# The linear half of four groups of up tiles by seven products instead of eight

## The chip, the cores and the metric

The kernel runs on one core of one Trainium2 chip. The metric is device time in microseconds (us), the median of several runs. The engines are PE (matrix products), DVE (elementwise, two operands), ACT (scalar engine: copies, activations), POOL (elementwise, off the main path) and SP (issues transfers).

## The reference

Two encoder layers over 512 tokens of width 1024. Each layer has a token mixer, a memory cross-attention, an output projection, and then a gated feed-forward part with a causal convolution of width 3 over the tokens. The change lies in this last part alone, `x + conv_ffn(rms_norm(x), ...)`:

```python
def conv_ffn(h, w_up, conv_w, conv_b, w_down):
    u = h @ w_up                                   # 512 x 1024 @ 1024 x 5632
    c = lax.conv_general_dilated(u, conv_w[:, None, :], ...) + conv_b
    a, g = jnp.split(c, 2, axis=-1)                # linear half, gate
    return (jax.nn.silu(g) * a) @ w_down           # 512 x 2816 @ 2816 x 1024
```

## The kernel before

Every float32 product is made of three matmuls on pieces: an operand is split into a high part (rounded by ACT) and a low part (the rest, by a subtraction on DVE), and PE adds high·high, high·low and low·high. So 128 weights by 512 tokens by one k tile of 128 are three matmuls of 512 columns (`product`, L387 to L389).

**Weights.** `_pieces` lists the weight pieces in the order of use, `_blocks` cuts them into blocks of up to 1024 columns. SP's queue loads a block into one of three `raw` tiles, `split_weights` makes `whi` (ACT, L255) and `wlo` (DVE, L258) of it; six such pairs exist (`WB`).

**The feed-forward part** works through 11 groups q of 256 linear columns ("ua") and 256 gate columns ("ug"), in parts of 4, 4 and 3 groups (`HALVES`). A group is two tiles n of 128 channels of each half; each tile is one PSUM bank of 128 channels x 512 tokens, summed over 8 k tiles, 24 matmuls. Its banks are taken in turn (`TURNS`, two each of mm, sm, lg, tp). `conv` then scales the bank by the row norms (DVE, L1165), takes one tap and the bias on ACT (L1167) and two taps on DVE (L1168, L1169). The gate passes SiLU (ACT, L1333), the halves are multiplied (DVE, L1334), and the result is split again for the product with `w_down` (ACT L1190, DVE L1191; tiles `mid`).

**The product with `w_down`** comes at the end of each part and is already done by a scheme of seven products in place of eight: k tiles are taken in pairs, channels in pairs, tokens in two halves of 256, and each of the seven products is three matmuls of 256 columns (`seven`, L1247), into four banks that `decode` (L1258 to L1266) puts together. It needs sums of weight quarters (`combined`: POOL L287 to L290 into `wsum`, split at L291 to L295) and sums of the groups' results (`combine`, L1198 to L1201, on POOL into `tsum`, for a part's last group on DVE; split at L1190 and L1191 into the tiles `mid2`). One channel block of 256 (c = 3 of layer 1) and all of layer 0's third part are done plainly.

**What sets the order.** PE runs in the order in which the code issues. The other engines' instructions are put in an order of their own by the framework's scheduler when the kernel is built; on each engine that order is fixed, so an instruction that waits holds up everything behind it there.

Of the kernel before, what the change touches and what calls it, by code (L numbers as in the profile page):

```python
# [11 lines left out]
F32 = mybir.dt.float32  # L12
# [9 lines left out]
S = 512  # L22
# [63 lines left out]
def _pieces():  # L86
# [6 lines left out]
    for l in range(2):  # L93
# [45 lines left out]

TURNS = ('mm', 'mm', 'sm', 'sm', 'lg', 'lg', 'tp', 'tp')  # L140
# [42 lines left out]
def trunk(ctx, tc, head_d, x_t, mem_t, wpack, cols_a_d, cols_d, conv_d, gate_d, rel_bias, diff_lambda, consts, onehot, out):  # L183
# [87 lines left out]
    done, raw_q = [0], deque()  # L271
# [6 lines left out]
    def combined(raw, n):  # L278
        pairs = n // 2
        full = lambda t: t[:, :512 * pairs].rearrange("p (j i c) -> p j i c", j=pairs, i=4)  # L280
        (h0, l0), (h1, l1) = [tuple(wp.tile([128, WTILE], F32R, name=t, tag=t, bufs=WB) for t in ("whi", "wlo"))
                              for _ in range(2)]
        r, wsum = full(raw), sum_pool[0].tile([128, WTILE], F32, name="wsum", bufs=2)
        a12, a22, a11, a21 = (r[:, :, i] for i in range(4))
        sv = wsum[:, :512 * pairs].rearrange("p (i j c) -> p i j c", i=4, j=pairs)
        s1, s2, s3, s4 = (sv[:, i] for i in range(4))
        ADD.tensor_add(s1, a21, a22)  # L287
        ADD.tensor_sub(s3, a11, a21)
        ADD.tensor_sub(s2, s1, a11)
        ADD.tensor_sub(s4, a12, s2)  # L290
        A.copy(full(h0)[:, :, :3], r[:, :, :3])  # L291
        V.tensor_sub(full(l0)[:, :, :3], r[:, :, :3], full(h0)[:, :, :3].bitcast(F32))
        m = slice(0, 512 * pairs)
        A.copy(h1[:, m], wsum[:, m])
        V.tensor_sub(l1[:, m], wsum[:, m], h1[:, m].bitcast(F32))  # L295
        out = []
        for j in range(pairs):
            own = lambda t, i: t[:, 512 * j + 128 * i:512 * j + 128 * i + 128]
            new = lambda t, i: t[:, 128 * (pairs * i + j):128 * (pairs * i + j) + 128]
# [3 lines left out]
        return out  # L303

    def make_block(raws=None):
# [9 lines left out]
        if plan[i][0][0] == "dn":  # L315
            made[i] += combined(raw, n)
# [8 lines left out]
    ADD = G  # L325


    def weights(key, by_block=False):
# [3 lines left out]
        if i + 1 < len(plan) and plan[i + 1][0][0] in ("dn", "dw"):  # L332
            limit = first_of[i + 1] + 1
# [814 lines left out]
    def ffn(pool, l, acc):  # L1148
        rB = pool.tile([128, S], F32, name="rB", bufs=1)
        sum_pool[0] = pool  # L1150
        old = list(zip(xh, xl))
        nu = [0]
# [4 lines left out]
        def up(parts, n, ops):  # L1157
            i = nu[0]
            nu[0] += 1
            p = bank(TURNS[i % 8])  # L1160
            product(p, parts, n, ops)
            return p

        def conv(p, j):
            V.tensor_mul(p, p, rB)  # L1165
            c = ctile()
            A.activation(c, p, AF.Identity, scale=cv[l][:, 2, j:j + 1], bias=cv[l][:, 3, j:j + 1])  # L1167
            V.scalar_tensor_tensor(c[:, 1:], p[:, :S - 1], cv[l][:, 1, j:j + 1], c[:, 1:], op0=ALU.mult, op1=ALU.add)  # L1168
            V.scalar_tensor_tensor(c[:, 2:], p[:, :S - 2], cv[l][:, 0, j:j + 1], c[:, 2:], op0=ALU.mult, op1=ALU.add)  # L1169
# [23 lines left out]
        left, right = blk(0, 256), blk(1, 256)  # L1193

        def combine(b2, b1, bh, bl, fh, fl, E):
            t = pool.tile([128, 2 * S], F32, name="tsum", bufs=1)
            q = [blk(i, 256) for i in range(4)]
            E.tensor_sub(t[:, q[0]], b1[:, right], b1[:, left])  # L1198
            E.tensor_sub(t[:, q[1]], b2[:, right], t[:, q[0]])
            E.tensor_sub(t[:, q[2]], b2[:, right], b1[:, right])  # L1200
            E.tensor_sub(t[:, q[3]], b2[:, left], t[:, q[1]])  # L1201
            h, lo = (pool.tile([128, 2 * S], F32R, name="mid2", bufs=9) for _ in range(2))
            for c in ((blk(0, S), blk(1, S)) if E is V else (blk(0, 2 * S),)):
                parts_of(t[:, c], h[:, c], lo[:, c])
            two = lambda hi, lw, c: (hi[:, c], lw[:, c])
            return [(fh, fl), two(bh, bl, left), two(bh, bl, right), two(h, lo, q[3]),
                    two(h, lo, q[0]), two(h, lo, q[1]), two(h, lo, q[2])]
# [4 lines left out]
        def down(base, nq, mids, pairs, tags, last, acc2):  # L1212
            first = used[0]
            whole = [plan[first + c][0][0] == "dw" for c in range(4)]
            sizes = [1 if plan[i][0][0] != "dn" else 2 for i, _, _ in order]
            live = sum(sizes[first_of[first]:done[0]])
            banks, seen = {}, [set() for _ in range(4)]

            def refill():
                nonlocal live  # L1220
                while done[0] < min(len(order), first_of[min(used[0] + 2, len(plan))]) and live + sizes[done[0]] <= WB:
                    live += sizes[done[0]]
                    make_block()

            def start(c):
                assert plan[used[0]][0][1:] == (l, base, c)
                used[0] += 1
                if whole[c] and l == 0:
                    banks[c] = [bank("lg"), bank("tp")]
                else:  # L1230
# [213 lines left out]
```

## Time and profile before

| | |
|---|---|
| median of 3 runs | 1149.71 us (1149.57 to 1151.2) |
| the profiled execution's own time | 1150.36 us |
| its span in the trace | 1148.5 us, granted clock 0.999 |
| PE busy | 1142.7 us, 99% |
| DVE busy | 871.2 us, 76% |
| ACT busy | 592.0 us, 52% |
| POOL busy | 193.2 us, 17% |

The spans of the trace leave about 1.9 us of the run's time outside. The feed-forward part of layer 0 lies at about 240 to 600 us, that of layer 1 at about 775 to 1144 us. A matmul's own span in the trace overlaps the next one's, so what a matmul costs is read from the distance of starts and not from its span. In groups of instructions the last two columns are busy time and mean of one, and the idle time ahead of them on that engine with what ended it.

### The profile page before, as it was taken

Reading aid. Unit: us, or ns where it says so; the run is one execution under the profiler, and the core shown is the slowest. Engines: PE = TensorE matmul, PEld = TensorE weight load, DVE = VectorE, ACT = ScalarE, POOL = GpSimd, SP = SyncE. Lnnn points to the kernel's source line nnn. Section 1 sums busy time; section 2 is a strip of 40 time slices with the busy share of each in tenths; the row PEclk is TensorE's granted clock in tenths of the full one; section 3 lists DMA queues with packets and bytes.
Section 4 is the critical chain, followed back from the end, with each engine's and each line's share of the span. In section 5 each row is a group of like instructions: output and inputs, shape, how many; then the busy total and the mean of one; then the engine's idle time right before and its main releaser. Section 6 shows DMA issues by size and latency. Waiting matters only on the chain.

```text
span 1148.5 us, 16655 instructions
## 1 busy us (share of the span) xinstructions
PE 1142.7 (99%) x6311; PEld 985.1 (86%) x6311; DVE 871.2 (76%) x1455; ACT 592.0 (52%) x1032; POOL 193.2 (17%) x230
## 2 busy tenths in 40 slices
PE   9999999999999999999999999999999999999998
PEld 7888888888899888988888888988888988899887
DVE  8576778688789677977677637777887977797777
ACT  6676686555454354434457634535644444453442
POOL 0000000001543125500000000000135403360340
PEclk9999999999999999999999999999999999999999
DMA  9522242133214322343252220333241342234212
GB/s 293 173 83 84 78 142 74 58 109 110 92 57 146 111 77 80 96 144 100 69 182 70 100 94 12 101 125 119 74 126 40 127 149 74 61 91 143 92 46 102
DMA packets 39662, 117.83 MB, mean 103 GB/s; under 512 B 4767, under 2 KB 7256, under 8 KB 39582
## 3 DMA queue, kind: packets, MB, share of 16 engines
q1 hardware_dynamic: 39150, 116.37, 31.8%
q8 instruction: 50, 0.82, 0.3%
q10 hardware_dynamic: 432, 0.39, 0.1%
q14 instruction: 30, 0.25, 0.1%
HBM read 112.54 MB, written 4.21 MB: 102 GB/s over the span
## 4 chain that ended last, share of the span: by engine, by line
PE 99%; DMA 0%; DVE 0%; ACT 0%; issue 0%
PE ps_mm L365 6%; PE ps_mm L367 6%; PE ps_mm L366 6%; PE ps_mm L387 6%; PE ps_mm L388 6%; PE ps_mm L389 6%; PE ps_lg L1247 5%; PE ps_sm L388 5%; PE ps_sm L389 5%; PE ps_sm L387 5%; PE ps_mm L1247 4%; PE ps_tp L388 4%; PE ps_lg L388 4%; PE ps_tp L387 4%; PE ps_lg L387 4%; PE ps_tp L389 4%
## 5 line engine op out<-in xcount | busy, mean ns | idle before, releaser
L258 DVE TENSOR_TENSOR wlo<-raw,whi 128x1024 fp32r<-128x1024 f32 (+4 forms) x174 | 194.2, 1127 | 77.0 <-ACT whi L255 76.4
L255 ACT CAST whi<-raw 128x1024 fp32r<-128x1024 f32 (+4 forms) x174 | 168.0, 976 | 124.2 <-PE ps_sm L388 29.8
L365 PE MATMUL ps_mm<-whi,xsh 128*128 128x512 f32 (+2 forms) x328 | 126.2, 385 | 0.0
L367 PE MATMUL ps_mm<-whi,xsl 128*128 128x512 f32 (+2 forms) x328 | 123.0, 375 | 0.0
L366 PE MATMUL ps_mm<-wlo,xsh 128*128 128x512 f32 (+2 forms) x328 | 122.8, 374 | 0.0
L387 PE MATMUL ps_mm<-xsh,whi 128*128 128x512 f32 x278 | 109.3, 393 | 0.0
L388 PE MATMUL ps_mm<-xsl,whi 128*128 128x512 f32 x278 | 108.4, 390 | 0.0
L389 PE MATMUL ps_mm<-xsh,wlo 128*128 128x512 f32 x278 | 108.2, 389 | 0.0
L387 PE MATMUL ps_sm<-xsh,whi 128*128 128x512 f32 x218 | 84.8, 389 | 0.0
L388 PE MATMUL ps_sm<-xsl,whi 128*128 128x512 f32 x218 | 84.8, 389 | 0.0
L389 PE MATMUL ps_sm<-xsh,wlo 128*128 128x512 f32 x218 | 84.8, 389 | 0.0
L365 PEld LDWEIGHTS ps_mm<-whi,xsh 128*128 128x128 f32 x328 | 61.7, 188 | 11.4 <-issue 1.0
L367 PEld LDWEIGHTS ps_mm<-whi,xsl 128*128 128x128 f32 x328 | 61.7, 188 | 11.3
L366 PEld LDWEIGHTS ps_mm<-wlo,xsh 128*128 128x128 f32 x328 | 61.8, 188 | 10.1
L387 PE MATMUL ps_lg<-xsh,whi 128*128 128x512 f32 x160 | 62.2, 389 | 0.0
L388 PE MATMUL ps_lg<-xsl,whi 128*128 128x512 f32 x160 | 62.2, 389 | 0.0
L389 PE MATMUL ps_lg<-xsh,wlo 128*128 128x512 f32 x160 | 62.2, 389 | 0.0
L387 PE MATMUL ps_tp<-xsh,whi 128*128 128x512 f32 x160 | 62.2, 389 | 0.0
L388 PE MATMUL ps_tp<-xsl,whi 128*128 128x512 f32 x160 | 62.2, 389 | 0.0
L389 PE MATMUL ps_tp<-xsh,wlo 128*128 128x512 f32 x160 | 62.2, 389 | 0.0
L389 PEld LDWEIGHTS ps_mm<-xsh,wlo 128*128 128x128 f32 x278 | 52.2, 188 | 11.0
L387 PEld LDWEIGHTS ps_mm<-xsh,whi 128*128 128x128 f32 x278 | 52.2, 188 | 10.8 <-issue 0.3
(382 smaller groups left out, 2835.4 us busy)
## 6 DMA issues: line engine op xcount, KB each, us to landing
raw<-in_wpack_dram SPq DMA_DIRECT2D x178, 512.0 KB, 3.5
xt<-in_x_t_dram SPq DMA_DIRECT2D x15, 256.0 KB, 5.2
raw<-in_wpack_dram SPq DMA_DIRECT2D x15, 256.0 KB, 3.1
raw<-in_wpack_dram SPq DMA_DIRECT2D x8, 384.0 KB, 3.0
xres<-xt SPq DMA_DIRECT2D x8, 256.0 KB, 3.2
xt<-xres SPq DMA_DIRECT2D x8, 256.0 KB, 5.8
out_dram<-xt SPq DMA_DIRECT2D x7, 256.0 KB, 2.0
bt<-bias_d SPq DMA_DIRECT2D x6, 256.0 KB, 4.1
```

What stands on the lines that cost most here:

```text
L255: ins = A.copy(hi[:, c], raw[:, c])
L258: V.tensor_sub(lo[:, c], raw[:, c], hi[:, c].bitcast(F32))
L365: mm(p, sh[k][:, blk(b)], hi, start=k == 0, stop=False)
L366: mm(p, sh[k][:, blk(b)], lo, start=False, stop=False)
L367: mm(p, sl[k][:, blk(b)], hi, start=False, stop=k == KT - 1)
L387: mm(p, hi[:, blk(n)], bh, start=i == first, stop=False)
L388: mm(p, hi[:, blk(n)], bl, start=False, stop=False)
L389: mm(p, lo[:, blk(n)], bh, start=False, stop=i == last)
L1247: mm(banks[c][b][:, h], w, v, start=b not in seen[c], stop=m == nq - 1 and t == 2 and i in close)
```

## The change

In both layers, for the groups 5, 6, 8 and 9 (eight pieces in all, `SEVEN`), the linear half's product with the tokens is done by the same scheme of seven. Of its 8 k tiles two (6 and 7) stay plain, and the six others form three pairs of seven products of three matmuls of 256 columns (`up_by_seven`). Both channel tiles of the piece come out together, from four banks; ACT copies half a bank, DVE makes four additions of 256 and two of 512 columns, and `conv` of both tiles follows. The gate's two tiles follow behind on PE.

The scheme needs sums of token halves for the three k pairs. They are made once a layer in groups 0 and 1 (`token_sums`, places in `SUMS_AT`): for each pair two scaled copies on ACT, four subtractions on POOL, and two splits of 512 columns on ACT and DVE. They stay in SBUF in 12 half-size tiles `vs`.

The weight sums of a block are issued one block ahead (`block_sums`, called from `ahead`), and POOL's additions are held in the order of the code. The operand splits of a group's result sums are not issued at once but behind the third `conv` that follows (`later`, `behind`); `tsum` is gone (its sums share `wsum`), and there are 8 `mid2` tiles in place of 9. The feed-forward part takes its banks in turn throughout (`take`), also in the product with `w_down`, and one count of live weight blocks (`live`, `refill`, `release`) governs their preparation across both products.

```diff
-                piece(("ua", l, q), "w_up", l, K8, (256 * q, 256 * q + 256))
-                piece(("ug", l, q), "w_up", l, K8, (DFF + 256 * q, DFF + 256 * q + 256))
+                for key, c in ((("ua", l, q), 256 * q), (("ug", l, q), DFF + 256 * q)):
+                    piece(key, "w_up", l, (6, 7, 4, 5, 0, 1, 2, 3) if key in SEVEN else K8, (c, c + 256))
...
+SEVEN = [("ua", l, q) for l in range(2) for q in (5, 6, 8, 9)]
+SUMS_AT = {1:(4,5),2:(0,1),3:(2,3)}
...
     def ahead():
...
+        i = order[done[0]][0] if done[0] < len(order) else None
+        if i is not None and by_seven(i) and done[0] not in summed:
+            summed[done[0]] = block_sums(raw_q[0], order[done[0]][1], int(plan[i][0][0] != "dn" and first_of[i] == done[0]))
+
+    def g_sums(items):
+        for op, o, x, y in items:
+            tc.keep_in_program_order(getattr(G, "tensor_" + op)(o, x, y))
...
+        def up_by_seven(i):
+            b, seen = take(4), set()
+            where = [(2, left), (0, left), (0, right), (1, left), (3, right), (2, right), (3, left)]
+            for m, ks in enumerate(((6, 7), (4, 5), (0, 1), (2, 3))):
+                while len(made) <= i or len(made[i]) <= m:
+                    refill()
+                part = made[i][m]
+                if m == 0:
+                    for n in range(2):
+                        product(b[n], part, n, [tokens[k] for k in ks], range(2), 99)
+                else:
+                    for r in steps:
+                        c, h = where[r]
+                        (hi, lo), (vh, vl) = part[r], sums_of[ks][r]
+                        for t, (w, v) in enumerate(((hi, vh), (hi, vl), (lo, vh))):
+                            mm(b[c][:, h], w, v, start=c > 1 and c not in seen, stop=m == 3 and t == 2 and r in (2, 5, 6, 3))
+                            seen.add(c)
+                if m % 2:
+                    release(i, 2, m == 3)
+            u, w = ctile(), ctile()
+            A.copy(u[:, left], b[2][:, left])
+            V.tensor_add(w[:, right], u[:, left], b[2][:, right])
+            V.tensor_add(u[:, right], w[:, right], b[3][:, right])
+            V.tensor_add(w[:, left], w[:, right], b[3][:, left])
+            V.tensor_add(w[:, right], u[:, right], b[3][:, left])
+            V.tensor_add(b[0], b[0], u)
+            V.tensor_add(b[1], b[1], w)
+            return b[:2]
...
+            if later:
+                convs[0] += 1
+                if convs[0] == 3:
+                    convs[0] = 0
+                    behind(first, final)
...
-            t = pool.tile([128, 2 * S], F32, name="tsum", bufs=1)
+            t = [ctile(), ctile()] if E is V else [sum_tile()]
...
+        def token_sums(ks):
+            (bh, bl), (fh, fl) = (tokens[k] for k in ks)
+            tiles = [split_tiles(pool, "vs", 12) for _ in range(2)]
...
+            combine(scaled(ks[0]), scaled(ks[1]), None, None, None, None, G, parts)
...
+                    if n == 0:
+                        at[key] = begin((key, l, q))
+                        if (key, l, q) in SEVEN:
+                            cs[key] = [conv(p, j + i) for i, p in enumerate(up_by_seven(at[key]))]
```

On PE, the start of group 5's linear piece in layer 0. Before (its first tile's bank is `ps_lg_4024`; `xsh` and `xsl` are the tokens' high and low parts, names with numbers are single buffers):

```order
L387 MATMUL ps_lg_4024<-xsh_2496,whi_3885 128x512
L388 MATMUL ps_lg_4024<-xsl_2497,whi_3885 128x512
L389 MATMUL ps_lg_4024<-xsh_2496,wlo_3886 128x512
L387 MATMUL ps_lg_4024<-xsh_2506,whi_3885 128x512
L388 MATMUL ps_lg_4024<-xsl_2507,whi_3885 128x512
L389 MATMUL ps_lg_4024<-xsh_2506,wlo_3886 128x512
```

It goes on like this for 24 matmuls, and then the gate's tile follows.

And the same piece now, where its plain products (L407 to L409) of the second tile end and the products by seven begin (L1233; `vsh` and `vsl` are token sums, the third bank is `ps_tp_4099`):

```order
L407 MATMUL ps_lg_4098<-xsh_2648,whi_3917 128x512
L408 MATMUL ps_lg_4098<-xsl_2649,whi_3917 128x512
L409 MATMUL ps_lg_4098<-xsh_2648,wlo_3918 128x512
L1233 MATMUL ps_lg_4097<-xsh_2564,whi_3917 128x256
L1233 MATMUL ps_lg_4097<-xsl_2565,whi_3917 128x256
L1233 MATMUL ps_lg_4097<-xsh_2564,wlo_3918 128x256
L1233 MATMUL ps_lg_4097<-xsh_2564,whi_3919 128x256
L1233 MATMUL ps_lg_4097<-xsl_2565,whi_3919 128x256
L1233 MATMUL ps_lg_4097<-xsh_2564,wlo_3920 128x256
L1233 MATMUL ps_tp_4099<-xsh_2588,whi_3917 128x256
L1233 MATMUL ps_tp_4099<-xsl_2589,whi_3917 128x256
L1233 MATMUL ps_tp_4099<-xsh_2588,wlo_3918 128x256
```

The first 12 matmuls of the piece are 512 columns wide, the 63 others 256, and the third bank is touched first after 12 + 6 of them.

On DVE, the `conv` of the same group's first linear tile. Before, with the operand split of group 4's sums (`mid_4009`) ahead of it and the gate's tile behind:

```order
L1165 TENSOR_TENSOR ps_lg<-ps_lg,rB 128x512
L1191 TENSOR_TENSOR mid_4009<-tsum,mid_4008 128x1024
L1168 SCALAR_TENSOR_TENSOR cvo<-ps_lg,cv_81,cvo 128x511
L1169 SCALAR_TENSOR_TENSOR cvo<-ps_lg,cv_81,cvo 128x510
L1165 TENSOR_TENSOR ps_lg<-ps_lg,rB 128x512
L1168 SCALAR_TENSOR_TENSOR cvo<-ps_lg,cv_81,cvo 128x511
L1169 SCALAR_TENSOR_TENSOR cvo<-ps_lg,cv_81,cvo 128x510
```

Now, from the additions (L1239 to L1244) on, with two weight splits (L309, L312) among them, then both linear tiles (`ps_lg`) and the gate's first (`ps_mm`):

```order
L1239 TENSOR_TENSOR cvo<-cvo,ps_tp 128x256
L1240 TENSOR_TENSOR cvo<-cvo,ps_tp 128x256
L1241 TENSOR_TENSOR cvo<-cvo,ps_tp 128x256
L309 TENSOR_TENSOR wlo<-raw,whi 128x2x384
L312 TENSOR_TENSOR wlo<-wsum,whi 128x1024
L1242 TENSOR_TENSOR cvo<-cvo,ps_tp 128x256
L1243 TENSOR_TENSOR ps_lg<-ps_lg,cvo 128x512
L1244 TENSOR_TENSOR ps_lg<-ps_lg,cvo 128x512
L1248 TENSOR_TENSOR ps_lg<-ps_lg,rB 128x512 x2
L1248 TENSOR_TENSOR ps_mm<-ps_mm,rB 128x512
L1251 SCALAR_TENSOR_TENSOR cvo<-ps_lg,cv_81,cvo 128x511 x2
L1252 SCALAR_TENSOR_TENSOR cvo<-ps_lg,cv_81,cvo 128x510 x2
```

The additions are new, the split of group 4's sums has gone behind these rows (four rows further down), and the gate's first scaling stands ahead of the linear tiles' last taps.

On DVE, the end of layer 0's second part (group 7 and the start of the product with `w_down`), from the last `conv` on. Before (the last group's sums at L1198 to L1201, both halves of their split in one row at the end):

```order
L292 TENSOR_TENSOR wlo<-raw,whi 128x2x384
L1165 TENSOR_TENSOR ps_tp<-ps_tp,rB 128x512
L295 TENSOR_TENSOR wlo<-wsum,whi 128x1024
L1168 SCALAR_TENSOR_TENSOR cvo<-ps_tp,cv_81,cvo 128x511
L1169 SCALAR_TENSOR_TENSOR cvo<-ps_tp,cv_81,cvo 128x510
L1334 TENSOR_TENSOR cvo<-cvo 128x512
L1198 TENSOR_TENSOR tsum<-cvo 128x256
L1200 TENSOR_TENSOR tsum<-cvo 128x256
L1199 TENSOR_TENSOR tsum<-cvo,tsum 128x256
L1191 TENSOR_TENSOR mid<-cvo,mid 128x256
L1201 TENSOR_TENSOR tsum<-cvo,tsum 128x256
L292 TENSOR_TENSOR wlo<-raw,whi 128x2x384
```

It goes on with the two halves of the split (`L1191 ... mid_4504<-tsum,mid_4503 128x512 x2`) and a weight split (L295). Now, from the first weight split behind the last `conv`'s scaling on:

```order
L312 TENSOR_TENSOR wlo<-wsum,whi 128x1024
L1251 SCALAR_TENSOR_TENSOR cvo<-ps_sm,cv_81,cvo 128x511
L1252 SCALAR_TENSOR_TENSOR cvo<-ps_sm,cv_81,cvo 128x510
L1448 TENSOR_TENSOR cvo<-cvo 128x512
L1287 TENSOR_TENSOR cvo<-cvo 128x256 x2
L1279 TENSOR_TENSOR mid<-cvo,mid 128x256
L1287 TENSOR_TENSOR cvo<-cvo 128x256
L309 TENSOR_TENSOR wlo<-raw,whi 128x2x384
L1287 TENSOR_TENSOR cvo<-cvo 128x256
L1279 TENSOR_TENSOR mid_4698<-cvo,mid_4697 128x512
L312 TENSOR_TENSOR wlo<-wsum,whi 128x1024
L1279 TENSOR_TENSOR mid_4698<-cvo,mid_4697 128x512
```

The weight split L312 now stands between the two halves of the last split (`mid_4698`). Ahead of the last scaling stands, in the order now, the operand split of group 6's sums (1024 columns), which before was 14 rows ahead of it.

More of the change, by code (lines that the diff above doesn't have):

```diff
@@ L285, in combined @@
[L285 to L293, printed above, removed]
+        if plain:
+            c = slice(0, 512 * plain + 384)
+            split_weights(c, raw, h0, l0)
+        else:
+            A.copy(full(h0)[:, :, :3], r[:, :, :3])
+            V.tensor_sub(full(l0)[:, :, :3], r[:, :, :3], full(h0)[:, :, :3].bitcast(F32))
@@ L314, in make_block @@
             made.append([])
-        if plan[i][0][0] == "dn":
-            made[i] += combined(raw, n)
+        if by_seven(i):
+            made[i] += combined(raw, summed.pop(done[0] - 1), n, int(plan[i][0][0] != "dn" and not made[i]))
         else:
@@ L1150, in ffn, with take, refill @@
         sum_pool[0] = pool
-        old = list(zip(xh, xl))
-        nu = [0]
+        tokens, sums_of, nb = list(zip(xh, xl)), {}, [0]
+        sizes = [2 if by_seven(i) else 1 for i, _, _ in order]
+        live = done[0] - first_of[used[0]]
+        left, right = blk(0, 256), blk(1, 256)
+        def take(n):
+            nb[0] += n
+            return [bank(TURNS[i % 8]) for i in range(nb[0] - n, nb[0])]
+        def refill():
+            nonlocal live
+            while done[0] < min(len(order), first_of[min(used[0] + 2, len(plan))]) and live + sizes[done[0]] <= WB:
+                live += sizes[done[0]]
+                make_block()
@@ L1217, in down @@
             banks, seen = {}, [set() for _ in range(4)]
[L1219 to L1223, printed above, removed]
-            def start(c):
[L1226 to L1230, printed above, removed]
-                    ta, tb = (("mm", "sm"), ("lg", "tp"))[(c + tags) % 2]
-                    banks[c] = [bank(t) for t in ((ta, tb) if whole[c] else (ta, ta, tb, tb))]
-                refill()
@@ L1235, in release, with emitted, seven @@
-            def release(c, m):
-                nonlocal live
-                piece = first + c
+            def start(c):
+                begin(("dw" if whole[c] else "dn", l, base, c))
+                banks[c] = take(2 if whole[c] else 4)
+            def emitted(c, m):
                 if m == nq - 1 or m % 2:
-                    live -= 1 if whole[c] else 2
+                    release(first + c, 1 if whole[c] else 2, m == nq - 1)
+            def seven(c, m, some=steps):
+                while len(made) <= first + c or len(made[first + c]) <= m:
@@ L1240, in release @@
                     refill()
-            def seven(c, m, some=steps):
                 for i in some:
```

175 lines of the change are left out of this document (115 added, 60 removed).

## Prediction

> **What bounds the kernel now.** I read the page's totals and the chain first, then the two feed-forward stretches and single groups by windows, then PE's starts.
>
> ```profile
> span 1148.5 us, 16655 instructions
> PE 1142.7 (99%) x6311; PEld 985.1 (86%) x6311; DVE 871.2 (76%) x1455; ACT 592.0 (52%) x1032; POOL 193.2 (17%) x230
> PE 99%; DMA 0%; DVE 0%; ACT 0%; issue 0%
> 240.00:600.00 360.00, 360.00 (x1928) 312.97 (x1927) 281.11 (x371) 166.41 (x217) 85.16 (x94) 1.00 0.33 106
> 775.00:1148.50 373.50, 369.01 (x2039) 323.33 (x2037) 297.37 (x401) 170.91 (x224) 104.67 (x121) 1.00 0.30 96
> 390.30:412.00 21.70, 21.70 (x97) 18.00 (x96) 16.51 (x22) 10.21 (x13) 3.06 (x4) 1.00 0.32 96
> 455.30:495.90 40.60, 40.60 (x339) 40.52 (x339) 37.80 (x51) 18.92 (x25) 18.95 (x20) 1.00 0.36 113
> 495.90:517.70 21.80, 21.80 (x99) 18.04 (x98) 16.75 (x23) 8.31 (x11) 0.00 (x0) 1.00 0.40 131
> 539.40:561.00 21.60, 21.60 (x97) 17.87 (x96) 14.88 (x21) 8.68 (x12) 0.42 (x1) 1.00 0.24 74
> 814.20:836.00 21.80, 21.80 (x98) 18.06 (x97) 19.72 (x27) 12.77 (x16) 3.05 (x4) 1.00 0.34 103
> ```
>
> The third row is the chain's; those behind it are windows and give the stretch, then busy time of PE, PE's weight loads, DVE, ACT, POOL, the clock and the transfers. PE is busy in the whole of layer 0's feed-forward part, and in layer 1's up to the 4.5 us tail of the last output, at full clock. So in these parts nothing but PE sets the time: what leaves PE is gained, as long as no other engine comes to hold it. The windows show how far they are from that: DVE has 16.51 of 21.70 us in group 5, 16.75 in group 8, 14.88 in group 10, and 37.80 of 40.60 in a product with `w_down` that already goes by seven.
>
> **PE's term.** The prices are read from distances of starts:
>
> ```profile
> 444.69 0.39 PE L387 MATMUL ps_tp<-xsh,whi 128*128 128x512 f32 x1
> 455.34 0.39 PE L389 MATMUL ps_tp<-xsh,wlo 128*128 128x512 f32 x1
> 455.57 0.40 PE L1247 MATMUL ps_mm<-mid,whi 128*128 128x256 f32 x2
> ```
>
> From 444.69 to 455.34 are 47 steps (two tiles of 24 matmuls): 0.2266 us for 512 columns. The product with `w_down` in the window from 455.30 is 4 channel blocks x 4 pairs x 21 = 336 matmuls of 256 columns, from 455.57 to 495.90: 0.1200 us. A piece is 48 x 0.2266 = 10.88 us before. Now it is 12 x 0.2266 + 63 x 0.1200 = 2.72 + 7.56 = 10.28 us. That removes 0.60 us, in eight pieces 4.8 us. The new products have the same shapes as L1247 (128 loaded columns, 256 streamed), so no other row is nearer. Reading errors of 1% in both prices would make it 5.5 at the most. Against the profiled execution (1150.36 us) this gives 1145.6; the median of before is 0.65 us under that execution, so against it 1144.9.
>
> **What DVE gets more.** Prices of one:
>
> ```profile
> L258 DVE TENSOR_TENSOR wlo<-raw,whi 128x1024 fp32r<-128x1024 f32 x143 | 172.7, 1219 | 70.7 <-ACT whi L255 70.2
> L258 DVE TENSOR_TENSOR wlo<-raw,whi 128x512 fp32r<-128x512 f32 x12 | 8.2, 681 | 2.5 <-ACT whi L255 2.5
> L295 DVE TENSOR_TENSOR wlo<-wsum,whi 128x1024 fp32r<-128x1024 f32 x35 | 47.9, 1368 | 1.5 <-ACT whi L294 1.3
> L292 DVE TENSOR_TENSOR wlo<-raw,whi 128x768 fp32r<-128x768 f32 x35 | 37.4, 1068 | 0.0
> L1260 DVE TENSOR_TENSOR cvo<-cvo,ps_tp 128x256 f32<-128x256 f32 x10 | 4.1, 410 | 0.0
> L1263 DVE TENSOR_TENSOR xt<-xt,ps_lg 128x512 f32<-128x512 f32 x10 | 6.8, 679 | 0.0
> L1169 DVE SCALAR_TENSOR_TENSOR cvo<-ps_lg,cv,cvo 128x510 f32<-128x510 f32 x20 | 15.0, 748 | 0.6
> L1190 ACT CAST mid<-cvo 128x256 fp32r<-128x256 f32 x16 | 6.5, 407 | 11.9 <-DVE cvo L1334 11.8
> L1198 DVE TENSOR_TENSOR tsum<-cvo 128x256 f32<-128x256 f32 x5 | 4.2, 846 | 0.2
> L287 POOL TENSOR_TENSOR wsum<-raw 128x256 f32<-128x256 f32 (+1 forms) x38 | 31.7, 835 | 135.1 <-DVE wlo L295 69.2 <-DMA raw<-in_wpack_dram 41.7 <-issue 24.2
> 422.13 1.36 DVE L1191 TENSOR_TENSOR mid<-tsum,mid 128x1024 fp32r<-128x1024 f32 x1 [3.20 <-ACT mid L1190]
> ```
>
> A piece's two weight splits (2 x 1.22) become four: 896 columns (about 1.09, between the rows of 512 and 1024), 512 (0.68), 768 (1.07), 1024 (1.37), so 1.8 us more. The additions are 4 x 0.41 + 2 x 0.68 = 3.0 us. So group 5 goes from 16.51 to 21.3 us of DVE and group 8 from 16.75 to 21.5, while PE's group shrinks from 21.76 to 21.16. DVE is full in groups 5, 6, 8 and 9, and works off its arrears in groups 7 and 10, which have 6 us to spare. The waiting is what decides then, not the sum. In its favour, DVE's worst waits go: the split of `tsum` stood at the head of DVE for 3.20 us at 422.13 until POOL and ACT had delivered, with the next `conv` behind it. Behind the third following `conv` its operands are long there. In before this wait cost PE nothing, so its end is worth nothing to PE, and it pays for the new work.
>
> How late may DVE be? A group takes 4 + 2 of the eight banks, so group 6's linear piece begins on two free banks and then takes the two of group 5's linear tiles. It needs the first of them after 12 wide and 6 narrow matmuls: 21.16 + 2.72 + 0.72 = 24.6 us after group 5's start. They come free with the last taps of group 5's `conv`. By the new order of DVE that is 10.28 (the product) + 0.5 (the copy on ACT, row L1190 and a hand-over) + the work up to the last tap. On DVE the next start comes some 0.08 us before a span ends (the two halves at 464.99, below, take 1.20 to the next start and 2 x 0.68 alone), so: 4 x 0.33 + 2 x 0.6 (additions), 1.0 + 1.3 (the two weight splits), 3 x 0.6 (scalings), 4 x 0.7 (taps), 9.4 together, and 20.2 us. That leaves 4.4 us. The same holds for group 9 behind group 8 and in layer 1: four places. The gate's banks come free earlier.
>
> **POOL, ACT and transfers.** A piece's sums are 4 additions of 128 columns and 4 of 256. With 0.84 us for the wide ones (row L287) and less for the narrow, 5 to 6 us more of POOL in groups where it had 3.06 (group 5) and 0.00 (group 8) of 21.7 us: hidden, except for what it does to DVE (below). POOL's fixed order puts a block's sums a whole block ahead; the piece's second block can be prepared from the end of the former linear piece on (10.3 us after its start) and is wanted at 21.2 + 5.2; POOL, ACT and DVE need about 6 us for it, so 10 us are left. SP loads the same blocks in the same order; a `raw` tile is read by one engine more, but earlier than by ACT, so I cost it at nothing, with that reserve as the cover. The token sums are, per layer, 12 subtractions on POOL (idle there but for 3.05 us in the row at 814.20), 12 instructions of about 0.6 us on ACT (12.77 of 21.80 busy) and 6 x 0.7 = 4.2 us on DVE. Group 1 of layer 1 has 19.72 of 21.80 of it and will overrun by about a microsecond, which group 2 takes back: a bank there comes round only after eight tiles, 43 us. Cost: nothing. All steps outside the feed-forward parts stay as they are.
>
> **The part ends.** Five times PE runs from the last up tile into products whose last operands DVE still makes.
>
> ```profile
> 456.91 0.69 DVE L1165 TENSOR_TENSOR ps_tp<-ps_tp,rB 128x512 f32<-128x512 f32 x1
> 460.92 1.05 DVE L1334 TENSOR_TENSOR cvo<-cvo 128x512 f32<-128x512 f32 x1 [0.76 <-ACT cvo L1333]
> 464.99 1.28 DVE L1191 TENSOR_TENSOR mid<-tsum,mid 128x512 fp32r<-128x512 f32 x2
> 466.19 1.21 DVE L295 TENSOR_TENSOR wlo<-wsum,whi 128x1024 fp32r<-128x1024 f32 x1
> 1113.87 0.69 DVE L1165 TENSOR_TENSOR ps_sm<-ps_sm,rB 128x512 f32<-128x512 f32 x1
> 1117.88 0.69 DVE L1334 TENSOR_TENSOR cvo<-cvo 128x512 f32<-128x512 f32 x1 [0.76 <-ACT cvo L1333]
> 1122.06 0.68 DVE L1191 TENSOR_TENSOR mid<-tsum,mid 128x512 fp32r<-128x512 f32 x1
> ```
>
> In group 7 PE starts `w_down` at 455.57 and wants the last operands after 63 + 21 + 9 + 9 = 102 narrow matmuls, 12.2 us later (467.8), their second half 0.7 us after that (468.5). They are there at 465.6 and 466.3 (464.99 and the two spans): 2 us of reserve. Now the weight split L312 (the 1.21 of L295 less 0.08) comes between the halves, and the second is 10.5 us behind the last scaling (9.4 before). That scaling began 1.3 us after PE was done, since DVE was late; with its long waits gone I expect 0.5. So the second half comes at 11.0 against 12.9. Layer 1's group 10 has 42 + 21 + 9 + 9 = 81 matmuls, 9.7 and 10.4 us; there the halves end 8.8 us behind the scaling (1113.87 to 1122.7) and the order between them is as before, so again 9 to 10 against 10.4. I take nothing for this and keep up to 1 us each as the other end.
>
> The sum: -4.8 and no new wait, 1144.9 us.
>
> **Rival 1: the part ends stall.** If DVE carries 2 to 3 us of arrears into the last scaling, the second half is late by 0.5 to 1 us at each of five ends: 2.5 to 5 us, 1147.4 to 1150. For it: the thin reserves, and 1.05 us for L1334 at 460.92 where the one at 1117.88 took 0.69, so there DVE is being slowed at just this place. Against it: groups 7, 3 and 10 have DVE to spare.
>
> **Rival 2: slower, by the bank of group 6 and 9.** DVE slows beside POOL: L1198's subtraction of 256 columns took 0.846 us on DVE where L1260, with one operand in PSUM, took 0.410. The Trainium skill, "SBUF — State Buffer", section "🔬 SBUF: two separate sides", calls the port pair of the two engines an exclusive lock: a DVE operation with two SBUF inputs and a GpSimd operation that reads SBUF do not share it, the loser blocks for the whole instruction. By that rule the sum would be the one of this rival only where the blocked time passes the reserve; the doubled L1198 agrees with it. In rows: about half of DVE's time in such a group is of that kind (splits, products of two `cvo`), so 6 us more of POOL cost DVE some 3 us up to the taps, 6 at the most. The reserve is 4.4 us. Four places at (lag - 4.4): a lag of 5.6 eats the gain, 7.5 makes 12.4 us, 1157.3. Against it: 3 us is under 4.4, POOL's additions are spread over the group, and three of DVE's waits have gone.
>
> **Rival 3: PE gets no cheaper.** Break-even is a narrow matmul at (36 x 0.2266) / 63 = 0.1295 us; then 1149.7. For it: the weight loads are 40.52 of 40.60 us busy with narrow matmuls, so their pace is the loads'. Against it: that very window has the 0.1200.
>
> **How the numbers follow.** The forecast's case has 0.67 and lies at 1143.9 to 1147.4. Rival 1 has 0.15, of which 0.03 stays under 1147.4. Rival 2 has 0.14, nearly all above 1152. Rival 3 has 0.04, half of it slower. A change under 0.2% (2.3 us) can hardly be told from none with this kernel's runs. Faster 0.70, same 0.14, slower 0.16. The range from 1143.9 (5.5 us of gain and a little) to 1151 leaves the stalls of rival 2 out.
>
> **What would show it.** Right: PE without idle in both parts, linear pieces of 10.3 us at groups 5, 6, 8 and 9, DVE above 95% there, no wait of the new split on ACT above 1 us. Wrong: PE waiting on DVE at the third bank of groups 6 and 9 (rival 2), on `mid2` some 10 to 12 us into `w_down` (rival 1), or narrow matmuls at 0.13 us (rival 3).

## The result and the profile after

The changed kernel takes 1153.09 us (median of 9 runs, 1152.47 to 1154.12) against 1149.72 us of the kernel before (9 runs): ratio 1.0028, 95% interval 1.0019 to 1.0036. It is slower by 3.4 us where 4.8 us of gain were forecast. So 8.2 us went somewhere.

The page of the changed kernel, span, busy times and the chain by engine, and then its two feed-forward stretches and five windows of layer 0 (stretch; PE, weight loads, DVE, ACT, POOL; clock, transfers): groups 5, 6, 8, 9 and 7.

```profile
span 1152.0 us, 17410 instructions
PE 1141.9 (99%) x6527; PEld 993.4 (86%) x6527; DVE 931.4 (81%) x1531; ACT 616.4 (54%) x1080; POOL 270.1 (23%) x318
PE 80%; DVE 13%; ACT 4%; issue 2%; POOL 1%; ACTq 0%; POOLq 0%; DVEq 0%
240.00:604.00 364.00, 360.64 (x2047) 318.08 (x2047) 312.11 (x410) 178.80 (x242) 122.99 (x139) 1.00 0.34 105
776.00:1152.00 376.00, 370.00 (x2155) 328.41 (x2154) 329.24 (x440) 184.51 (x249) 144.23 (x165) 1.00 0.31 97
392.18:413.36 21.18, 21.18 (x124) 18.82 (x123) 16.71 (x23) 9.90 (x14) 7.82 (x9) 1.00 0.34 100
413.36:434.54 21.18, 21.18 (x124) 18.83 (x123) 19.22 (x28) 10.85 (x15) 5.89 (x8) 1.00 0.37 109
499.88:521.09 21.21, 21.21 (x125) 18.83 (x124) 19.54 (x29) 8.73 (x11) 7.91 (x8) 1.00 0.39 123
521.09:542.27 21.18, 21.18 (x124) 18.82 (x123) 19.52 (x28) 11.71 (x16) 0.00 (x0) 1.00 0.46 137
434.54:456.30 21.76, 21.76 (x97) 18.02 (x96) 20.35 (x27) 11.43 (x16) 6.53 (x9) 1.00 0.28 88
```

The gain on PE is there: the four groups by seven take 21.18 to 21.21 us where they took 21.76, 0.6 us less each, and PE is busy all through them. But the chain, 99% PE before, is 80% PE and 13% DVE now. PE's busy time in layer 0's feed-forward part is 360.64 of 364.00 us where it had no idle at all. The next view is what PE waited for (us in total, times, longest), and behind it PE's starts at the end of layer 0's second part.

```profile
PE ps_tp L1359 <- DVE mid L1279: 3.2, 4, 1.3
PE ps_sm L1359 <- DVE mid L1279: 2.7, 4, 0.8
468.67 0.39 PE L1359 MATMUL ps_tp<-mid,whi 128*128 128x256 f32 x1 [1.27 <-DVE mid L1279]
470.81 0.39 PE L1359 MATMUL ps_tp<-mid,whi 128*128 128x256 f32 x1 [0.44 <-DVE mid L1279]
472.55 0.38 PE L1359 MATMUL ps_tp<-mid,whi 128*128 128x256 f32 x1 [0.76 <-DVE mid L1279]
```

All new waits are of one kind: products with `w_down` that wait for the last group's operand splits. The view counts a wait only from the modelled end of the matmul ahead. By starts (a product of 336 matmuls should last 335 x 0.12 us from its first start to its last) the ends at groups 3 and 7 of layer 0 and at groups 3, 7 and 10 of layer 1 lose 1.40, 3.26, 2.71, 1.15 and 0.37 us: 8.9 us. That covers the missing time: the profiled execution took 1153.93 us, 9.0 us over the forecast, the median 8.2 us. There is no wait on a bank anywhere.

DVE at that place, the end of layer 0's second part (PE leaves the last up tile at 456.30), and behind it a sum on POOL and the cast on ACT that the weight split at 461.79 waits for:

```profile
453.12 0.69 DVE L1248 TENSOR_TENSOR ps_sm<-ps_sm,rB 128x512 f32<-128x512 f32 x1
...
458.32 1.75 DVE L1279 TENSOR_TENSOR mid<-wsum,mid 128x1024 fp32r<-128x1024 f32 x1
460.00 0.69 DVE L1248 TENSOR_TENSOR ps_sm<-ps_sm,rB 128x512 f32<-128x512 f32 x1
461.79 1.37 DVE L312 TENSOR_TENSOR wlo<-wsum,whi 128x1024 fp32r<-128x1024 f32 x1 [1.10 <-ACT whi L311]
...
465.36 1.16 DVE L1448 TENSOR_TENSOR cvo<-cvo 128x512 f32<-128x512 f32 x1 [0.76 <-ACT cvo L1446]
466.56 1.72 DVE L1287 TENSOR_TENSOR cvo<-cvo 128x256 f32<-128x256 f32 x2
468.20 0.41 DVE L1279 TENSOR_TENSOR mid<-cvo,mid 128x256 fp32r<-128x256 f32 x1
468.54 0.41 DVE L1287 TENSOR_TENSOR cvo<-cvo 128x256 f32<-128x256 f32 x1
...
470.68 1.22 DVE L312 TENSOR_TENSOR wlo<-wsum,whi 128x1024 fp32r<-128x1024 f32 x1
471.81 0.68 DVE L1279 TENSOR_TENSOR mid<-cvo,mid 128x512 fp32r<-128x512 f32 x1
...
456.14 1.44 POOL L285 TENSOR_TENSOR wsum<-raw 128x256 f32<-128x256 f32 x2 [3.49 <-DVE wlo L312]
...
460.71 1.05 ACT L311 CAST whi<-wsum 128x1024 fp32r<-128x1024 f32 x1 [3.55 <-POOL wsum L285]
```

The last scaling (460.00) begins 3.7 us after PE's last up tile: DVE is already late there, and group 6's split of sums (458.32, 1.75 us) stands right ahead of it. Behind it the weight split waits 1.10 us for POOL and ACT, the product and the first two sums run slowed (1.16 us, and 0.86 each where one takes 0.41 at 468.54), and a weight split stands between the halves. From the scaling's start to the end of the second half it is 12.5 us; before it was 9.4.

### The profile page after: what moved, and what is told of

Read it like the earlier page. It is cut to its first block, busy times and chain, and to the rows that moved or that the text cites. A ratio compares the mean times of both kernels' runs of the same rounds, so it can differ in the third digit from the quotient of the medians.

```text
span 1152.0 us, 17410 instructions
## 1 busy us (share of the span) xinstructions
PE 1141.9 (99%) x6527; PEld 993.4 (86%) x6527; DVE 931.4 (81%) x1531; ACT 616.4 (54%) x1080; POOL 270.1 (23%) x318
## 4 chain that ended last, share of the span: by engine, by line
PE 80%; DVE 13%; ACT 4%; issue 2%; POOL 1%; ACTq 0%; POOLq 0%; DVEq 0%
PE ps_mm L385 6%; PE ps_mm L408 6%; PE ps_mm L407 6%; PE ps_mm L409 6%; PE ps_mm L387 6%; PE ps_mm L386 6%; PE ps_lg L1359 3%; PE ps_sm L408 3%; PE ps_sm L407 3%; PE ps_sm L409 3%; PE ps_mm L1359 3%; PE ps_tp L224 3%; PE ps_lg L1233 3%; PE ps_tp L1359 2%; PE ps_sm L1359 2%; DVE mid L1279 2%
## 5 line engine op out<-in xcount | busy, mean ns | idle before, releaser
L260 DVE TENSOR_TENSOR wlo<-raw,whi 128x1024 fp32r<-128x1024 f32 (+5 forms) x166 | 188.7, 1148 | 74.7 <-ACT whi L257 73.8
L257 ACT CAST whi<-raw 128x1024 fp32r<-128x1024 f32 (+5 forms) x166 | 157.9, 967 | 104.9 <-PE ps_mm L408 24.3
L407 PE MATMUL ps_mm<-xsh,whi 128*128 128x512 f32 x310 | 121.8, 393 | 0.0
L408 PE MATMUL ps_mm<-xsl,whi 128*128 128x512 f32 x310 | 120.9, 390 | 0.0
L409 PE MATMUL ps_mm<-xsh,wlo 128*128 128x512 f32 x310 | 120.8, 390 | 0.0
L285 POOL TENSOR_TENSOR wsum<-raw 128x256 f32<-128x256 f32 (+1 forms) x108 | 87.8, 834 | 117.5 <-DMA raw<-in_wpack_dram 64.1
L1287 POOL TENSOR_TENSOR wsum<-cvo 128x256 f32<-128x256 f32 x40 | 33.9, 848 | 226.7 <-DVE cvo L1448 140.9
L407 PE MATMUL ps_sm<-xsh,whi 128*128 128x512 f32 x202 | 78.6, 389 | 0.0
L409 PE MATMUL ps_sm<-xsh,wlo 128*128 128x512 f32 x202 | 78.6, 389 | 0.0
L312 DVE TENSOR_TENSOR wlo<-wsum,whi 128x1024 fp32r<-128x1024 f32 (+1 forms) x54 | 70.6, 1307 | 8.9 <-ACT whi L311 8.9
L311 ACT CAST whi<-wsum 128x1024 fp32r<-128x1024 f32 (+1 forms) x54 | 51.9, 962 | 39.8 <-POOL wsum L285 39.5
L409 PEld LDWEIGHTS ps_mm<-xsh,wlo 128*128 128x128 f32 x310 | 58.2, 188 | 12.1
L407 PEld LDWEIGHTS ps_mm<-xsh,whi 128*128 128x128 f32 x310 | 58.2, 188 | 11.9 <-issue 0.3
L408 PEld LDWEIGHTS ps_mm<-xsl,whi 128*128 128x128 f32 x310 | 58.3, 188 | 11.9 <-DVE xsl L366 0.4
```

What stands on the lines that cost most here:

```text
L257: ins = A.copy(hi[:, c], raw[:, c])
L260: V.tensor_sub(lo[:, c], raw[:, c], hi[:, c].bitcast(F32))
L285: tc.keep_in_program_order(getattr(G, "tensor_" + op)(o, x, y))
L407: mm(p, hi[:, blk(n)], bh, start=i == first, stop=False)
L408: mm(p, hi[:, blk(n)], bl, start=False, stop=False)
L409: mm(p, lo[:, blk(n)], bh, start=False, stop=i == last)
```

## The experiments

Two numbers per part end carry all that follows: the **lag**, from PE's first matmul of the product with `w_down` to DVE's last scaling of the part, and the **tail**, from the start of that scaling to the end of the last half of `mid2`. Both are differences of starts and ends in the trace. In a part of four groups PE wants the last half after 108 narrow matmuls, 12.96 us.

Theory A: the change's new order on DVE lengthens lag and tail by itself, whatever PE's new pieces do. Theory B: the pieces by seven fill DVE, and its arrears arrive at the part's end.

**Without the pieces by seven.**

```diff
-SEVEN = [("ua", l, q) for l in range(2) for q in (5, 6, 8, 9)]
-SUMS_AT = {1:(4,5),2:(0,1),3:(2,3)}
+SEVEN = []
+SUMS_AT = {}
```

> Leaves the up tiles plain (no piece by seven, no token sums) and keeps the rest of the change: weight sums a block ahead, operand splits behind the third conv, the new bank turns. Theory A (the tail of each part is delayed by the new order alone: the late operand split ahead of the last scaling, the weight split's wait and its place between the halves): PE waits on mid2 at all five part ends as in the changed kernel at groups 3 (1.4 and 2.7 us), 1.4 to 3 us at groups 7, together 6 to 10 us, so 1155.5 to 1159.5 us. Theory B (DVE arrives late at the part ends because the pieces by seven fill it): waits only at groups 3, none at groups 7 and 10, 1149.7 to 1154 us.

Measured: 1152.69 us, ratio 1.0027 (1.0017 to 1.0036). PE waits 0.7 us at each of the four-group ends and 0.4 at group 10, 3.1 us in all. It is slower than before with nothing of the gain in it, so theory B alone is out. But 3.1 us are half of the least that theory A asked for; at equal tail (12.5 us) the lag here is 1.1 us everywhere, in the changed kernel 1.8, 3.7, 3.2, 1.6. DVE at the end of group 7 of layer 0, where PE leaves the up tiles at 456.24:

```profile
455.68 1.76 DVE L1279 TENSOR_TENSOR mid<-wsum,mid 128x1024 fp32r<-128x1024 f32 x1
457.37 0.69 DVE L1248 TENSOR_TENSOR ps_tp<-ps_tp,rB 128x512 f32<-128x512 f32 x1
459.15 1.37 DVE L312 TENSOR_TENSOR wlo<-wsum,whi 128x1024 fp32r<-128x1024 f32 x1 [1.10 <-ACT whi L311]
...
469.18 0.68 DVE L1279 TENSOR_TENSOR mid<-cvo,mid 128x512 fp32r<-128x512 f32 x1
```

**Splits behind the second conv.** One digit:

```diff
-                if convs[0] == 3:
+                if convs[0] == 2:
```

> The changed kernel with the operand splits behind the second following conv in place of the third; in the new order of DVE the split then stands ahead of the third conv's scaling, and the weight split between the halves moves behind both. Theory A: the waits on mid2 at the four ends of four groups fall from 8.6 us to under 2 us, 1144.5 to 1147 us. Theory B: the waits go at groups 3 (4.1 us) but stay at groups 7 (4.4 us), 1149 us.

Measured: 1144.57 us, ratio 0.9955 (0.9942 to 0.9967). Not one wait on `mid2` is left. Its page (span, busy times, chain), and DVE at the end of layer 0's second part, where PE leaves the up tiles at 454.48:

```profile
span 1142.7 us, 17419 instructions
PE 1138.5 (100%) x6527; PEld 991.8 (87%) x6527; DVE 930.2 (81%) x1531; ACT 617.4 (54%) x1080; POOL 290.0 (25%) x318
PE 99%; DMA 0%; DVE 0%; issue 0%; SPq 0%; ACT 0%
447.00 1.61 DVE L1279 TENSOR_TENSOR mid<-wsum,mid 128x1024 fp32r<-128x1024 f32 x1
...
456.16 0.68 DVE L1248 TENSOR_TENSOR ps_sm<-ps_sm,rB 128x512 f32<-128x512 f32 x1
456.76 1.21 DVE L312 TENSOR_TENSOR wlo<-wsum,whi 128x1024 fp32r<-128x1024 f32 x1
...
461.37 2.06 DVE L1287 TENSOR_TENSOR cvo<-cvo 128x256 f32<-128x256 f32 x3
...
464.89 1.28 DVE L1279 TENSOR_TENSOR mid<-cvo,mid 128x512 fp32r<-128x512 f32 x2
```

The split of group 6's sums now lies 9 us ahead of the last scaling, the lag is 1.7 us and the tail 10.0, together 11.7 of 12.96. The weight split has moved behind both halves, and the other one no longer waits. Theory A's forecast is met, and the time is the predicted one of the change (1144.9) within 0.4 us.

**Splits at once, and behind the first conv.** The first issues `parts_of(x, ...)` in place of `later.append((x, ...))`, the second has `convs[0] == 1`.

> The changed kernel with the operand splits issued at once, as before the change. Theory A: the tail is short again, so the waits at groups 3 go (4.1 us); DVE waits 2 to 4 us for each split again, which in the groups by seven makes it late by as much, under the 4.4 us of the bank reserve: 1144.9 to 1149 us. Theory B: the late DVE carries more into groups 7, and PE waits there 3 us or more each, 1151 us or more.

Measured: 1157.11 us, ratio 1.0063 (1.0049 to 1.0076). The time is in theory B's range, but not for its reason: PE loses 5.3 and 4.8 us at groups 3 and only 1.5 and 1.4 at groups 7.

> The changed kernel with the operand splits behind the first following conv. The arrears theory (PE pays what DVE's last scaling comes after PE's end of the part's last up tile, plus the tail behind it, less 13.0 us at a four-group part): the tail is the short one of 10.0 us, as the split and the second weight split stand as behind the second conv, but the split comes before POOL and ACT have its operands, so DVE waits 1 to 2 us per group at its head, and the last scalings come 3 to 5 us late: waits of 0 to 2 us at each of four ends, 1145 to 1150 us. If head waits of that size are absorbed: 1144.6 us.

Measured: 1152.39 us, ratio 1.0023 (1.0014 to 1.0032). Both expectations missed the size. DVE waits at its head again, for the splits' casts 27.7 us in all at once and 14.2 behind the first conv, where it is 4.8 in the changed kernel and 2.1 behind the second conv. Here are such waits in layer 0 for the split of group 2's sums (at once) and of group 1's (behind the first conv):

```profile
323.73 1.36 DVE L1279 TENSOR_TENSOR mid<-wsum,mid 128x1024 fp32r<-128x1024 f32 x1 [2.50 <-ACT mid L1278]
```

```profile
304.47 1.35 DVE L1279 TENSOR_TENSOR mid<-wsum,mid 128x1024 fp32r<-128x1024 f32 x1 [1.67 <-ACT mid L1278]
```

The tails are short (9.3 us), but the lags at groups 3 are 7.6 and 7.0 us at once, 7.2 and 6.6 behind the first conv. I had expected 3 to 5 us of them at the most. At groups 7 the lags are 5.0 and 4.8, then 3.4 and 3.4, and only the former make PE wait. So the place of the splits has a narrow best value: at once 1157.1, one conv 1152.4, two 1144.6, three 1153.1 us.

**Neither pieces by seven nor the late split** (`SEVEN = []`, no sums, second conv).

> No piece by seven, and the operand splits behind the second conv: the order of the changed kernel without both suspects. Theory A: PE is as long as before and the waits at the part ends are under 2 us in all, 1149.7 to 1151.5 us. Theory B: the same within 1 us, as nothing fills DVE; it tells how much of the rest of the change costs anything by itself.

Measured: 1149.33 us, ratio 0.9996 (0.9987 to 1.0005). No wait, lag 0.5, tail 10.0, as at the end of group 7 of layer 0, where PE leaves the up tiles at 455.87:

```profile
456.41 0.68 DVE L1248 TENSOR_TENSOR ps_tp<-ps_tp,rB 128x512 f32<-128x512 f32 x1
...
465.14 1.28 DVE L1279 TENSOR_TENSOR mid<-cvo,mid 128x512 fp32r<-128x512 f32 x2
```

All that the change does beside the two suspects costs nothing that can be measured. The third conv in place of the second adds, without pieces, 0.6 us of lag and 2.5 of tail. And 1149.33 - 1144.57 = 4.8 us is what eight pieces by seven are worth, as worked out beforehand.

**Token sums alone.** (`SEVEN = []`, `SUMS_AT` as in the change, third conv; nothing reads the sums.)

> No piece by seven, but the token sums are still made (nothing reads them); operand splits behind the third conv. Theory A2 (behind the last scaling of a part the new order takes 12.5 us in place of 9.4, which uses up the reserve, and from there each microsecond that DVE is late is paid by PE; DVE is late at groups 3 from the token sums and at groups 7 and 10 from the pieces by seven): waits at groups 3 as in the changed kernel (1.4 and 2.7 us), at groups 7 and 10 as without any (0.7, 0.7, 0.4), together 5.9 over the 1149.3 of the order behind the second conv: 1155.2 us. Theory B2 (the token sums are absorbed long before group 3; what is late there is late for another reason, such as the new turns of banks): as without them, 1152.7 us.

Measured: 1155.62 us, ratio 1.005 (1.0037 to 1.0062), as theory A2 has it. Lag and tail at the five ends, with the earlier runs:

| | group 3 | group 7 | group 3, layer 1 | group 7, layer 1 | loss of all five |
|---|---|---|---|---|---|
| before | 2.4 + 9.4 | 1.3 + 9.4 | 1.9 + 9.3 | 1.4 + 9.4 | 0 |
| changed | 1.8 + 12.5 | 3.7 + 12.5 | 3.2 + 12.5 | 1.6 + 12.5 | 8.9 |
| no pieces, no sums | 1.1 + 12.5 | 1.1 + 12.5 | 1.1 + 12.5 | 1.1 + 12.5 | 3.1 |
| sums alone | 1.8 + 12.5 | 1.1 + 12.5 | 3.2 + 12.5 | 1.1 + 12.5 | 5.9 |
| second conv | 1.9 + 10.0 | 1.7 + 10.0 | 2.3 + 10.0 | 1.7 + 10.0 | 0 |

At every end in the table the loss by starts is lag + tail - 12.96 within 0.1 us, or nothing where that is negative. The losses of all five include group 10 of layer 1, at most 0.4 us. The token sums of groups 0 and 1 are still felt at group 3 (0.7 and 2.1 us of lag), the pieces by seven at group 7 (2.6 and 0.5 us). Neither costs PE anything while the tail is 10 us.

**The second conv in a part's last group alone.**

```diff
-                if convs[0] == 3:
+                if convs[0] == (2 if at_end[0] else 3):
...
+                at_end[0] = q == base + nq - 1
```

> The changed kernel, with the splits behind the second conv in the last group of each part alone, behind the third in all others. Theory A2: only the tail of the part counts, so 1144.6 us within 0.5, as with the second conv everywhere. If the late splits of the other groups are what makes DVE late, waits of 2 us or more remain: 1146.5 us or more.

Measured: 1145.13 us, ratio 0.996 (0.9948 to 0.9973), with one wait of 0.2 us at group 3 of layer 1, where the lag is 3.0 us against 2.3 with the second conv everywhere. So 8.0 of the 8.5 us that the second conv brings come from the splits of the parts' last groups; those of the other groups show only in this lag.

**A third tile for the sums.** (`wsum` with `bufs=3`, on the kernel without pieces and sums. In the changed kernel the token sums take the room for it, so this was run without them only.)

> No piece by seven and no token sums, operand splits behind the third conv, and three tiles for the sums in place of two (there is room for a third only without the token sums). Theory ring (the late split holds one of two tiles, so the next block's sums on POOL start late and DVE waits 1.1 us for them behind the last scaling): that wait goes, the tail falls from 12.5 to some 11.3 us, PE's waits from 3.2 to under 0.5 us: 1149.3 to 1149.9 us. Theory order (the place of the split and of the weight split alone): waits stay over 2 us, 1151.5 to 1153 us.

Measured: 1151.18 us, ratio 1.0013 (1.0004 to 1.0022), between the two. DVE's weight split behind the last scaling, and the work behind it:

```profile
458.34 1.21 DVE L312 TENSOR_TENSOR wlo<-wsum,whi 128x1024 fp32r<-128x1024 f32 x1
...
462.95 1.73 DVE L1287 TENSOR_TENSOR cvo<-cvo 128x256 f32<-128x256 f32 x2
464.60 0.95 DVE L1279 TENSOR_TENSOR mid<-cvo,mid 128x256 fp32r<-128x256 f32 x1
465.48 0.95 DVE L1287 TENSOR_TENSOR cvo<-cvo 128x256 f32<-128x256 f32 x1
```

The wait of 1.10 us is gone, but the tail falls from 12.5 to 12.2 us alone: operations that take 0.41 us in the changed kernel (468.20 and 468.54 above) now take 0.95, as POOL's sums run beside them. So the ring of two tiles was the cause of the wait, but not of the tail's length: most of the wait came back as slowed work. PE still loses 0.4 us at each of the four ends; at group 10 it loses nothing, as the lag there fell from 1.1 to 0.2 us. What is left between 12.2 and the 10.0 of the second conv is the weight split between the halves (1.1 us) and this slowing (1.1 us).

**Weight sums not a block ahead**, with the third and with the second conv. `ahead` no longer calls `block_sums`, `make_block` does.

```diff
...
-            made[i] += combined(raw, summed.pop(done[0] - 1), n, int(plan[i][0][0] != "dn" and not made[i]))
+            plain = int(plan[i][0][0] != "dn" and not made[i])
+            made[i] += combined(raw, block_sums(raw, n, plain), n, plain)
```

> The changed kernel (splits behind the third conv), with a block's weight sums issued when the block is made and not a block ahead. If the advance itself loads the tail with POOL's work and a waiting weight split (1.1 us of wait, 1 us of slowed DVE work per end): the tail falls from 12.5 to about 11, PE's waits from 9 to 4 us or less, 1147 to 1150 us. If the advance is what keeps DVE from waiting for POOL and ACT at its head: DVE waits more for the weight sums, last scalings come later, waits of 9 us or more: 1153 us or more.

Measured: 1187.51 us, ratio 1.0326 (1.0311 to 1.0341).

> Splits behind the second conv, and the weight sums not ahead. With the advance harmless and useless: 1144.6 us. With the advance needed: DVE waits for sums at its head in the groups by seven and at the part ends, 1146 us or more.

Measured: 1171.11 us, ratio 1.0182 (1.0168 to 1.0197). The advance is needed, by 26 us, and again the part ends pay: by starts the five lose 26.1 us, in part in waits on the weight splits themselves, with lags of 6.7 to 9.8 us at the four-group ends. DVE in group 5 of the latter:

```profile
406.56 0.69 DVE L309 TENSOR_TENSOR wlo<-wsum,whi 128x512 fp32r<-128x512 f32 x1 [3.77 <-ACT whi L308]
...
412.10 1.23 DVE L309 TENSOR_TENSOR wlo<-wsum,whi 128x1024 fp32r<-128x1024 f32 x1 [2.52 <-ACT whi L308]
```

Two splits of weight sums wait 6.3 us at DVE's head in one group, with the additions of the piece behind them.

**More pieces**, with the second conv: groups 4 of both layers and group 10 of layer 0, and then group 10 of layer 0 alone.

```diff
-SEVEN = [("ua", l, q) for l in range(2) for q in (5, 6, 8, 9)]
+SEVEN = [("ua", l, q) for l in range(2) for q in (4, 5, 6, 8, 9)] + [("ua", 0, 10)]
```

> Splits behind the second conv, and three more pieces by seven: group 4 in both layers and group 10 in layer 0. Where DVE still keeps up: 3 x 0.6 us less than 1144.6, so 1142.8 us. Where three such groups in a row (4, 5, 6) make DVE late by more than the 4.4 us of the bank reserve or by more than the 1.3 us that are left at the end of group 7: 1144 to 1148 us, with waits on a bank or on mid2.

Measured: 1144.48 us, ratio 0.9954 (0.9941 to 0.9968). The lag at groups 7 rises to 3.4 and 3.5 us and PE waits 1.3 us there in all; the three pieces, 1.8 us by their price, bring hardly more than they cost.

> Splits behind the second conv, and group 10 of layer 0 by seven as well, the one group that no product with sums follows. PE gains one piece, 0.6 us, and no deadline lies behind the group: 1144.0 us within 0.3. If it fills DVE where layer 1 or the plain product needs it: 1144.6 us or more.

Measured: 1144.15 us, ratio 0.9949 (0.9937 to 0.9962), 0.4 us under the second conv without it, where 0.6 were expected; the intervals of the two overlap. It is the lowest median of all that was run.

## Why the prediction was wrong

- **PE's term was right.** A piece takes 10.28 us (starts at 392.18 and 402.46 in the changed kernel), the groups 0.6 us less each, and the pieces' worth by two runs that differ in nothing else to PE is 4.8 us. Rival 3 is out. (Reading errors of 1% in opposite directions would have made it 6.0 us, not 5.5; nothing came to depend on that.)
- **DVE's added work was right too** for the pieces: 931.4 - 892.7 = 38.7 us of busy time (the changed kernel against the token sums alone), where eight times 4.8 are 38.4.
- **The part ends were wrong, and that decided it.** This is the step that failed: the sum took no wait for them, and they cost 8.9 us. It put the last scaling 0.5 us behind PE and the second half 10.5 us behind that, 11.0 against 12.9. They are 3.7 and 12.5 in group 7 of layer 0, 16.2 in all. In layer 1's group 10, where it set 9 to 10 against 10.4, it is 10.6. Of the tail's 2.0 us too much, 1.1 are the wait of the weight split for its sums at 461.79, and 0.9 are slowed work. Both come with POOL's sums, which run under the tail until 468.0, 11.7 us behind PE's last up tile (before, 7.0 us), and of which the step took no account. The weight split between the halves (1.1 us) had been seen and was rightly sized.
- **The lag** of 0.5 us failed at every four-group end: it is 1.6 to 3.7 us. The split behind the third conv comes in the last group right ahead of the last scaling and takes 1.7 us there. I had shown that place myself, gave it no cost, and expected the vanished head waits to shorten the lag. But the place accounts for little of it: without pieces the lag is 1.1 us with the third conv and 0.5 with the second, and with the pieces it is still 1.7 to 2.3 with the second. The rest are arrears of the token sums and the pieces that do reach the end, as the table shows. Groups 7 were said to have 6 us to spare, and DVE is busy 20.35 of 21.76 us in group 7 of layer 0. The windows of groups 5, 6, 8 and 9 are not as full as the prediction had it: DVE is busy 16.7 to 19.5 of 21.2 us there, and not 21. It waits at its head, and work moves on into later windows; the longest such waits in groups 5 and 6 are 1.72 us for the cast of weight sums and 1.85 us for that of `mid`. No run took these waits away, so how much of the lag is theirs stays open:

```profile
406.44 1.23 DVE L312 TENSOR_TENSOR wlo<-wsum,whi 128x1024 fp32r<-128x1024 f32 x1 [1.72 <-ACT whi L311]
428.38 0.90 DVE L1279 TENSOR_TENSOR mid<-cvo,mid 128x256 fp32r<-128x256 f32 x1 [1.85 <-ACT mid L1278]
```

- **Rival 1 was the right mechanism** with a price of 2.5 to 5 us; it measured 8.9. Its sign came too: PE waits on the last group's splits from 12 us into the product. It counted 0.5 to 1 us an end for lags of 2 to 3 us, which with its own tail of 10.5 would be 0.6 at the most; with the true tail the same lags give 1.5 to 2.5 us each. What spoke against it, that groups 7 and 3 have DVE to spare, did not hold.
- **Token sums at nothing** was right only where the tail has reserve. They are taken back by group 2 as far as banks go, but not as far as the part's end goes: 0.7 and 2.1 us of lag at groups 3, 2.9 us of time between the two kernels without pieces (1155.62 and 1152.69). They also take more of DVE than was counted: it is busy 892.7 us with them and 879.0 without, 13.7 us more where 8.4 were counted.
- **Rival 2 did not come.** No run showed a wait on a bank. The last taps of group 5's linear tiles ended at 413.62, 21.4 us after the group's start where 20.2 were counted, and PE took the third bank of group 6 at 416.80, so 3.2 of the 4.4 us were left:

```profile
412.22 1.40 DVE L1252 SCALAR_TENSOR_TENSOR cvo<-ps_lg,cv,cvo 128x510 f32<-128x510 f32 x2
416.80 0.28 PE L1233 MATMUL ps_lg<-xsh,whi 128*128 128x256 f32 x1
```

  The slowing that it rests on is there: the subtraction of two `cvo` took 0.86 us each at 466.56 while POOL ran and 0.41 at 468.54, after POOL's last sum:

```profile
467.20 0.79 POOL L285 TENSOR_TENSOR wsum<-raw,wsum 128x256 f32<-128x256 f32 x1
```

  The Trainium skill's rule on the shared port pair ("SBUF — State Buffer", section "🔬 SBUF: two separate sides") agrees with these rows. It struck not the bank but the part's tail.
- **One block ahead at nothing** was right, and more: without it 26 us are lost.

## What to carry to other kernels

A deferral that takes a wait off the head of a queue must be judged at the place where the queue has a deadline: here one position decided between 0.9955 and 1.0028, and the best place was the last at which operands are ready and the deadline is not yet in the way. For each such deadline, add lag and tail and compare them with the time that the waiting engine still has work for; below it arrears cost nothing, above it every microsecond counts in full. Where a helper slows the engine that it serves, as POOL's sums slow DVE here (0.95 us beside them, 0.41 alone), a wait that is removed by starting the helper earlier may come back as slowed work.

## What the runs showed of the hardware

Short waits of PE can cost its clock. With the splits at once, PE waited twice 1.3 us and some shorter times between 336.6 and 343.1, and then issued narrow matmuls every 0.213 us where 0.120 is normal, until 347.0. Windows of that run (columns as above; the granted clock is the third number from the end):

```profile
343.60:346.90 3.30, 3.30 (x18) 3.30 (x17) 3.30 (x5) 0.78 (x2) 0.21 (x1) 0.50 0.40 120
347.00:360.00 13.00, 13.00 (x110) 13.00 (x110) 12.58 (x17) 6.67 (x8) 12.84 (x11) 1.00 0.39 118
```

That is 3.4 us at half clock, some 1.5 us lost beside the waits; the same came at group 3 of layer 1. The Trainium skill, "TensorE: Matmul & The Clock Gate", section "What's actually happening", describes such a gate, with an observation window of about 3.4 us and half the clock after an idle one; length and ratio agree with these rows, but here PE was waiting for only part of the time before, by starts 3.6 of the 6.5 us. The changed kernel's own waits at group 7 of layer 0, 3.2 of the 5.4 us from 467.1 to 472.5, left the clock at 1.00. So the share of waiting alone does not decide it, and what does stays open.
